# A bidirectional mLSTM layer on Trainium2: the head norm moved into the output stage, per head and 512 tokens

## The chip, the cores and the metric

The kernel runs on one core of a Trainium2 chip. The metric is the device time of one execution in microseconds (us); the median of the runs shown before the change is 2925.31 us. The engines are TensorE (PE; its weight loads are shown as PEld), VectorE (DVE), ScalarE (ACT), GpSimd (POOL) and SyncE (SP), which issues nearly all DMAs.

## The reference

One encoder layer is applied to two sequences that share all weights: a prompt of 1024 tokens and a sample of 2048 tokens, model width 1024. 16 learned meta tokens are put ahead of each. Everything is float32.

```
xn   = rmsnorm(h) ; proj = xn @ w_in + b_in          # 1024 -> 6672 columns
ya   = neighbourhood_attention(na_q, na_k, na_v) * silu(na_z) @ w_a
q, k = split(silu(conv3(ml_qk)))                     # 4 heads of 128
hm   = mlstm(q, k, v, gates) forward + the same backward
hm   = sigmoid(ml_o) * hm
hm   = (hm - mean(hm)) * rsqrt(var(hm) + eps)        # over the 128 of one head
yb   = (hm * head_g * silu(ml_z)) @ w_b
y    = (sigmoid(ga) * ya + sigmoid(gb) * yb) @ w_out
out  = h + rmsnorm(y)
```

The change concerns the three lines from `sigmoid(ml_o)` to `head_g * silu(ml_z)`: the output gate, the norm over one head, the head weights and the second gate.

## The kernel before

Two generators are woven into one program. The **dense** side does the projections and the final blocks: PLAN lists groups of columns for 1024 tokens (m: mLSTM columns, n: attention columns, g: merge gates) and, marked "f", final blocks of 512 tokens. The order is prompt m and n, sample m and n, prompt g, the prompt's final blocks f(0,0) and f(0,1), the rest of the sample, then f(1,0) to f(1,3). The **sparse** side does, in this order, the prompt's mLSTM, the prompt's neighbourhood attention (NA), the sample's mLSTM, the sample's NA. Every `yield` of the sparse side names how many us of dense PE work are to be put in before it goes on (A_D in the states stage, A_A in the output stage, A_N in the norm stage, A_NA in NA). PE executes in exactly this written order. The order of DVE, ACT and SP is chosen when the program is built; each of these engines then also runs in its order, so a waiting instruction holds back those behind it.

Every float32 product is made of three matmuls with operands split into a high and a low part (L144 to L146, L412 to L414, L1305 to L1307). The weights' parts stream from DRAM through four buffers (`whi`, `wlo`, issued at L231 when a buffer comes free). A projection unit ends in a pj bank of PSUM (three of them), which ACT or DVE evacuates; results go to DRAM (`mk`, `mq`, `nk`, ...), and the sparse side loads them again. The first group of a half of 512 tokens also stores its activation parts (`xh`, `xl`, L317).

The mLSTM of a sequence runs per head: `ml_states` (yields A_D) walks backwards over blocks of 256 tokens and leaves the chunk states, and `ml_outputs` (4 + 6 x (NB + 1) yields of A_A for NB blocks, NB being 4 or 8) walks forward. In each of its steps of six yields it makes the scores of block b (`scores`, `scores_lo`, with decay masks `um` loaded from DRAM), the products of block b - 1 with the states and with v (`back`: PE into banks tr and sm, ACT to `tt`, DVE adds into `num`), and `finish` divides by `den` into `hb`, stored to H in DRAM. The parts `vh`, `vl` of v (in `kv`) and `cch`, `ccl` of the states (in `state`) have two buffers each and are made a block ahead.

After all four heads, `ml_norm` runs as a stage of its own (1 + 5 N + 2 yields of A_N, N being 4 or 8, at 717 to 771 us for the prompt and 1930 to 2014 us for the sample): it loads H, TO (tanh of half the output gate) and SZ (the second gate) for 128 tokens and all heads, gates (L1179), takes means and variances (L1181, L1183), the inverse root (`rsqrt8`, L126 to L136), normalises (L1193), multiplies by SZ (L1194), transposes on PE (L1205), and ACT copies (L1206) to `ybo`, which is stored to YB. The head weights are in SZ already: `tm_store` multiplies each projected tile of SZ by them (L438; `hgb`, loaded in `tm_unit`).

A final block begins with `yload`, which loads YA and YB and splits them (ACT L1248, DVE L1249). It is started during the previous final block, one piece after each of its 16 output tiles, once NA and mLSTM have marked the 512 tokens done; if they never do in that time, the block loads at its own start.

```
            while acc > 0.0:
                d = next(dense, None)
...
                    elif self.ready(*nxt[1:]):
                        hook = self.yload(*nxt[1:])
```

Of the kernel before, what the change touches and what calls it, by code (L numbers as in the profile page):

```python
# [9 lines left out]
F32 = mybir.dt.float32  # L10
# [97 lines left out]
A_NA, A_D, A_A, A_N, A_G = 1.52, 1.63, 1.63, 1.85, 1.3  # L108


class K:
# [55 lines left out]
    def setup2(self):  # L167
# [10 lines left out]
        nc.vector.tensor_scalar(self.cw[:, 12:24], self.cw[:, 12:24], S_K, None, op0=ALU.mult)  # L178
        self.ones = cp.tile([P, P], F32, name="ones")
# [9 lines left out]
        self.H = [t(f"h{s}", [SEQLEN[s], 512]) for s in range(2)]  # L189
# [197 lines left out]
    def tm_unit(self, col, halves, wd):  # L387
# [4 lines left out]
        if C_MZ <= col < C_MO:  # L392
            hg = wp.tile([P, 1, 256], F32, name="hgb", bufs=1)
            nc.sync.dma_start(hg[:, 0, :], _bc(self.i["head_g"], col - C_MZ, wd))
            nc.vector.tensor_scalar(hg, hg, -0.125, None, op0=ALU.mult)
            self.hgt = hg
# [29 lines left out]
    def tm_store(self, col, wd, s, n, cnt, tok, st):  # L426
# [6 lines left out]
        if C_MZ <= col < C_MO:  # L433
# [3 lines left out]
            for a in range(2):  # L437
                nc.vector.tensor_tensor(st[:, a, :wd], st[:, a, :wd], self.hgt[:, 0, :], op=ALU.mult)  # L438
# [422 lines left out]
    def ml(self, s):  # L861
        tc, nc = self.tc, self.nc
        T = SEQLEN[s]
        NB = T // BL
        with tc.tile_pool(name=f"mg{s}", bufs=1, side="right", reuse_waits="tile") as keep:
            with tc.tile_pool(name=f"mt{s}", bufs=1, side="right", reuse_waits="tile") as mp:
                self.tri = keep.tile([P, 2, P], F32, name="tri")
                nc.sync.dma_start(self.tri, self.i["tri"])
                self.trim = keep.tile([P, 2, CB, P], F32, name="trim")
                for j in range(CB):  # L870
                    nc.sync.dma_start(self.trim[:, :, j, :], self.i["trimask"])
                g = []
                yield from self.ml_gates(s, keep, mp, g)
            with tc.tile_pool(name=f"ml{s}", bufs=1, side="right", reuse_waits="tile") as mp:
                self.vas = [mp.tile([P, CB, 130], F32, name=f"va{j}") for j in range(3)]
                for va in self.vas:
                    nc.gpsimd.memset(va[:, :, 128:129], 1.0)
                    nc.gpsimd.memset(va[:, :, 129:130], 0.0)
                for h in range(4):
                    sts = {}  # L880
                    yield from self.ml_states(mp, s, h, g, NB, sts)
                    yield from self.ml_outputs(mp, s, h, g, NB, sts)
        with tc.tile_pool(name=f"mn{s}", bufs=1, side="right", reuse_waits="tile") as mp:
            yield from self.ml_norm(mp, s)
# [103 lines left out]
    def ml_outputs(self, mp, s, h, g, NB, sts):  # L988
# [3 lines left out]
        raws, kfs, vas, ums, convs, qs, kss, vs, shs, cs, nums = ({} for _ in range(11))  # L992

        def load(b):
            if b < NB:
# [6 lines left out]
                for d in range(2):  # L1002
                    um = mp.tile([P, CB, P], F32, name="um", bufs=4)
                    ud = self.UD[s][d]
                    src = bass.AP(tensor=ud.tensor, offset=ud.offset + ((1 + b * CB) * 4 + h) * P, ap=[[0, P], [4 * P, CB], [1, P]])
                    nc.sync.dma_start(um, src)
                    ums[b].append(um)

# [19 lines left out]
        def kv(b):  # L1028
            if b < NB:
                kf, va = kfs.pop(b), vas.pop(b)  # L1030
# [4 lines left out]
                vh = mp.tile([P, CB, 130], F32R, name="vh", bufs=2)  # L1035
                vl = mp.tile([P, CB, 130], F32R, name="vl", bufs=2)
                nc.scalar.activation(f2(vh), f2(va), AF.Copy)
                nc.vector.tensor_tensor(f2(vl), f2(va), f2(vh).bitcast(F32), op=ALU.subtract)
                kss[b], vs[b] = (kh, kl), (vh, vl)
# [8 lines left out]
        def state(b):  # L1048

            if b < NB:  # L1050
                for j in range(CB):
# [5 lines left out]
                cch = mp.tile([P, CB, 260], F32R, name="cch", bufs=2)  # L1057
                ccl = mp.tile([P, CB, 260], F32R, name="ccl", bufs=2)
# [22 lines left out]
        def back(b, j):  # L1081
# [6 lines left out]
            tt = mp.tile([P, 2, 130], F32, name="tt", bufs=1)  # L1088
            for d in range(2):
                nc.scalar.activation(tt[:, d], pi[:, 130 * d:130 * d + 130], AF.Copy, scale=g[d]["e"][:, cc, h:h + 1])  # L1090
# [3 lines left out]
            if j == 0:  # L1094
                nums[b] = mp.tile([P, CB, 2, 130], F32, name="num", bufs=1)
            num = nums[b]
            nc.vector.tensor_tensor(num[:, j].rearrange("p d c -> p (d c)"), pa[:, :260], tt.rearrange("p d c -> p (d c)"), op=ALU.add)

        def finish(b):
# [27 lines left out]
        state(0)  # L1127
        yield A_A
        for b in range(NB + 1):
            p = b - 1  # L1130
            if b < NB:
                scores(b)
                conv_a(b + 1)
# [19 lines left out]
            state(b + 1)  # L1153
            yield A_A

    def ml_norm(self, mp, s):

        nc = self.nc
        N = SEQLEN[s] // (2 * P)
        ld, hs, rr = {}, {}, {}  # L1160

        def load(i):
            if i < N:
                ld[i] = []
                for e in range(2):
                    rows = slice((2 * i + e) * P, (2 * i + e + 1) * P)
                    hb = mp.tile([P, 4, P], F32, name="hn", bufs=6)
                    to = mp.tile([P, 4, P], F32, name="tog", bufs=4)
                    sz = mp.tile([P, 4, P], F32, name="szg", bufs=4)
                    for x, dr in ((hb, self.H), (to, self.TO), (sz, self.SZ)):  # L1170
                        nc.sync.dma_start(x.rearrange("p a b -> p (a b)"), dr[s][rows, :])
                    ld[i].append((hb, to, sz))

        def stats(i):
            bs = mp.tile([P, 2, 4, 6], F32, name="bs", bufs=2)
            mv = mp.tile([P, 2, 4, 2], F32, name="mv", bufs=2)
            for e in range(2):
                hb, to, _ = ld[i][e]
                nc.vector.scalar_tensor_tensor(hb, to, 1.0, hb, op0=ALU.add, op1=ALU.mult)  # L1179
                for h in range(4):  # L1180
                    nc.vector.bn_stats(bs[:, e, h], hb[:, h])  # L1181
                for h in range(4):
                    nc.vector.bn_aggr(mv[:, e, h], bs[:, e, h])  # L1183
                yield A_N
            ve = mp.tile([P, 2, 4], F32, name="ve", bufs=2)
            nc.vector.tensor_scalar(ve, mv[:, :, :, 1], 4.0 * EPS, None, op0=ALU.add)
            rr[i] = mv, self.rsqrt8(mp, ve, [P, 2, 4])

        def norm(i, e):
            mv, r = rr[i]  # L1190
            hb, _, sz = ld[i][e]
            for h in range(4):
                nc.vector.tensor_scalar(hb[:, h], hb[:, h], mv[:, e, h, 0:1], r[:, e, h:h + 1], op0=ALU.subtract, op1=ALU.mult)  # L1193
            nc.vector.tensor_tensor(hb, hb, sz, op=ALU.mult)  # L1194

        def turn(i, e):
            if i < 0:
                return
            hb = ld[i][e][0]
            if e == 0:  # L1200
                rr[i] = mp.tile([P, 4, 2, P], F32, name="ybo", bufs=2)
            yo = rr[i]
            pt = self.psum("tr", [P, 4, P])
            for h in range(4):
                nc.tensor.transpose(pt[:, h, :], hb[:, h], self.ident)  # L1205
            nc.scalar.activation(yo[:, :, e, :], pt, AF.Copy)  # L1206
            if e:
                for h in range(4):
                    nc.sync.dma_start(self.YB[s][h][:, 2 * P * i:2 * P * (i + 1)], yo[:, h].rearrange("p a b -> p (a b)"))
                ld.pop(i)  # L1210
                rr.pop(i)

        load(0)
        yield A_N
        for i in range(N + 1):
            if i < N:
                load(i + 1)
                yield from stats(i)
                yield A_N
            turn(i - 1, 0)  # L1220
            if i < N:
                norm(i, 0)
            yield A_N
            turn(i - 1, 1)
            if i < N:
                norm(i, 1)
            yield A_N
        self.done.add(("ml", s))
# [265 lines left out]
```

## Time and profile before

| what | value |
|---|---|
| median of three runs (lowest to highest) | 2925.31 us (2923.33 to 2926.53) |
| the profiled execution: its time, its span | 2927.06 us, 2925.1 us |
| PE busy, DVE busy, ACT busy (share of the span) | 97%, 60%, 44% |
| mean granted TensorE clock | 0.986 |
| DMA queue q1, share of 16 engines | 669.41 MB, 70.0% |

The span runs from the first to the last instruction of the profiled execution; the rest of its time lies around that. Busy times are unions over an engine's instructions. Matmuls are pipelined and their ends are modelled, so PE's 97% says that PE is nearly always occupied, not that it is at its peak. Where PE is not waiting, a 512-column matmul starts every 0.23 us, a 256-column one every 0.12 us.

### The profile page before, as it was taken

Reading aid. Unit: us, or ns where it says so; the run is one execution under the profiler, and the core shown is the slowest. Engines: PE = TensorE matmul, PEld = TensorE weight load, DVE = VectorE, ACT = ScalarE, POOL = GpSimd, SP = SyncE. Lnnn points to the kernel's source line nnn. Section 1 sums busy time; section 2 is a strip of 40 time slices with the busy share of each in tenths; the row PEclk is TensorE's granted clock in tenths of the full one; section 3 lists DMA queues with packets and bytes.
Section 4 is the critical chain, followed back from the end, with each engine's and each line's share of the span. In section 5 each row is a group of like instructions: output and inputs, shape, how many; then the busy total and the mean of one; then the engine's idle time right before and its main releaser. Section 6 shows DMA issues by size and latency. Waiting matters only on the chain.

```text
span 2925.1 us, 49552 instructions
## 1 busy us (share of the span) xinstructions
PE 2824.3 (97%) x17488; PEld 2514.2 (86%) x17488; DVE 1745.3 (60%) x4722; ACT 1287.4 (44%) x3114; POOL 23.0 (1%) x107
## 2 busy tenths in 40 slices
PE   6999999999799999899999999999999999999998
PEld 6998898899689988798887998888888888979877
DVE  5233566556556765466558786565555557786843
ACT  4112546443344444356566554523444445544421
POOL 1000000000000000000000000000000000000000
PEclk9999999999899999999999999999999999999999
DMA  9655566755775654469669898578569659797875
GB/s 348 222 174 184 194 224 235 251 180 195 254 248 155 200 167 142 138 219 312 212 213 356 279 346 281 154 261 273 178 190 298 192 163 289 249 303 242 274 245 194
DMA packets 438760, 675.26 MB, mean 231 GB/s; under 512 B 52240, under 2 KB 253024, under 8 KB 438512
## 3 DMA queue, kind: packets, MB, share of 16 engines
q1 hardware_dynamic: 437392, 669.41, 70.0%
q0 software_dynamic: 1120, 2.69, 0.4%
q8 instruction: 138, 2.26, 0.3%
q14 instruction: 110, 0.90, 0.1%
HBM read 455.05 MB, written 216.90 MB: 230 GB/s over the span
## 4 chain that ended last, share of the span: by engine, by line
PE 82%; DMA 9%; DVE 5%; ACT 1%; SPq 1%; issue 1%; ACTq 0%; DVEq 0%
PE pj L144 14%; PE pj L145 14%; PE pj L146 14%; PE pj L412 6%; PE pj L413 6%; PE pj L414 6%; PE pj L1305 3%; PE pj L1307 3%; PE pj L1306 3%; PE sm L702 3%; PE tr L690 3%; DMA tg<-gt 1%; PE sc L665 1%; PE sc L666 1%; PE sm L146 1%; DMA um<-ud 1%
## 5 line engine op out<-in xcount | busy, mean ns | idle before, releaser
L144 PE MATMUL pj<-xh,whi 128*128 128x512 f32 (+1 forms) x1824 | 722.3, 396 | 1.0 <-DVE xl L310 1.0
L145 PE MATMUL pj<-xl,whi 128*128 128x512 f32 (+1 forms) x1824 | 702.3, 385 | 0.1
L146 PE MATMUL pj<-xh,wlo 128*128 128x512 f32 (+1 forms) x1824 | 700.5, 384 | 0.0
L412 PE MATMUL pj<-whi,xh 128*128 128x256 f32 (+3 forms) x1576 | 451.0, 286 | 0.0
L413 PE MATMUL pj<-wlo,xh 128*128 128x256 f32 (+3 forms) x1576 | 444.6, 282 | 0.0
L414 PE MATMUL pj<-whi,xl 128*128 128x256 f32 (+3 forms) x1576 | 444.1, 282 | 0.0
L146 PEld LDWEIGHTS pj<-xh,wlo 128*128 128x128 f32 x1824 | 345.5, 189 | 72.3
L144 PEld LDWEIGHTS pj<-xh,whi 128*128 128x128 f32 x1824 | 346.0, 190 | 55.9 <-DVE xl L310 1.2
L145 PEld LDWEIGHTS pj<-xl,whi 128*128 128x128 f32 x1824 | 346.5, 190 | 53.2 <-DVE xl L310 0.4
L412 PEld LDWEIGHTS pj<-whi,xh 128*128 128x128 f32 (+1 forms) x1576 | 294.3, 187 | 1.2
L413 PEld LDWEIGHTS pj<-wlo,xh 128*128 128x128 f32 (+1 forms) x1576 | 294.0, 187 | 1.0
L414 PEld LDWEIGHTS pj<-whi,xl 128*128 128x128 f32 (+1 forms) x1576 | 293.9, 187 | 0.9
L673 ACT ACTIVATE prb<-sc,mx 128x384 f32<-128x384 f32 (+2 forms) x192 | 120.1, 625 | 237.4 <-DVE mx L669 236.3
L1305 PE MATMUL pj<-whi,mh 128*128 128x256 f32 x768 | 221.7, 289 | 2.7 <-DVE yo L1333 2.7
L1307 PE MATMUL pj<-whi,mlo 128*128 128x256 f32 x768 | 217.7, 283 | 0.0
L1306 PE MATMUL pj<-wlo,mh 128*128 128x256 f32 x768 | 217.4, 283 | 0.0
L669 DVE CUSTOM_DVE_ANT_1 sc<-sc,gt 128x384 f32<-128x384 f32 (+2 forms) x192 | 118.9, 619 | 96.3 <-PE sc L666 86.8
L708 DVE TENSOR_TENSOR yg<-sm,yg 64x128 f32<-64x128 f32 x384 | 108.4, 282 | 108.0 <-ACT yg L706 100.2
L421 DVE TENSOR_TENSOR stT<-pj,bb 128x256 f32<-128x256 f32 (+3 forms) x197 | 83.2, 422 | 143.8 <-PE pj L414 142.7
L144 PE MATMUL pj<-yh,whi 128*128 128x512 f32 x384 | 158.3, 412 | 8.5 <-ACT yh L1248 6.1
L693 DVE TENSOR_TENSOR pts<-tr,pts 96x512 fp32r<-96x512 f32 (+2 forms) x192 | 131.6, 685 | 47.8 <-ACT pts L692 46.0
L145 PE MATMUL pj<-yl,whi 128*128 128x512 f32 x384 | 153.9, 401 | 0.2 <-DVE yl L1249 0.2
(234 smaller groups left out, 5074.6 us busy)
## 6 DMA issues: line engine op xcount, KB each, us to landing
whi<-wh SPq DMA_DIRECT2D x176, 512.0 KB
wlo<-wl SPq DMA_DIRECT2D x176, 512.0 KB
wh<-whi SPq DMA_DIRECT2D x64, 512.0 KB
wl<-wlo SPq DMA_DIRECT2D x64, 512.0 KB
wraw<-w_in SPq DMA_DIRECT2D x48, 512.0 KB
gt<-st SPq DMA_DIRECT2D x96, 256.0 KB
tg<-gt SPq DMA_DIRECT2D x96, 256.0 KB
xh<-xh SPq DMA_DIRECT2D x6, 2048.0 KB
```

The lines of the kernel that those rows point to most:

```text
L144: mm(out, ah, bh, start=start, stop=False)
L145: mm(out, ah, bl, start=False, stop=False)
L146: mm(out, al, bh, start=False, stop=stop)
L412: nc.tensor.matmul(o, xh, wh, start=k == 0, stop=False)
L413: nc.tensor.matmul(o, xh, wl, start=False, stop=False)
L414: nc.tensor.matmul(o, xl, wh, start=False, stop=k == KT - 1)
L669: nc.vector.tensor_tensor_reduce(out=so, in0=so, in1=gt[:, g0:g0 + ns, c0:c0 + 32], op0=ALU.add, op1=ALU.min, scale=-1.0, scalar=3.0e38, a ...
L673: nc.scalar.activation(pr_[:, :N].rearrange("p (b a c) -> p b a c", b=4, c=8), sc[:, :N].rearrange("p (a b c) -> p b a c", b=4, c=8), AF.E ...
L693: nc.vector.tensor_tensor(pts[:ks, :, 1, :], pt[:ks], pts[:ks, :, 0, :].bitcast(F32), op=ALU.subtract)
L1305: nc.tensor.matmul(o, mh[:, k, xs], wh, start=k == 0, stop=False)
L1306: nc.tensor.matmul(o, mh[:, k, xs], wl, start=False, stop=False)
L1307: nc.tensor.matmul(o, ml[:, k, xs], wh, start=False, stop=k == KT - 1)
```

## The change

The norm stage is dissolved. `finish` now collects two blocks (512 tokens) of one head in `hb`, and every second block hands a small generator `ml_norm` to a queue. Each further yield of the output stage, or of the next head's states, runs one step of it: gate and statistics, inverse root, normalise and second gate, two empty steps, then four transposes, one ACT copy and one store to YB. TO and SZ are loaded per head and 512 tokens (`gates`), in pieces of 512 bytes a row. H is gone.

The head weights are no longer multiplied into SZ: they are a per-partition scale (`hg`, times -0.125) of the ACT copy behind the transposes, where a partition is a channel of the head.

`back` lets ACT write the state part straight into `num`, and DVE adds in place (`tt` is gone). `vh`, `vl`, `cch` and `ccl` have one buffer each and are made in the last yield of the block that they belong to, `state(b)` instead of `state(b + 1)`; the split of v moves there from `kv`. A_A is 1.9 instead of 1.63, A_N is gone. The removed lines are the old `ml_norm`, `hgb` and L438, described above.

```diff
-A_NA, A_D, A_A, A_N, A_G = 1.52, 1.63, 1.63, 1.85, 1.3
+A_NA, A_D, A_A, A_G = 1.52, 1.63, 1.9, 1.3
...
+        self.hg = cp.tile([P, 4], F32, name="hg")
+        nc.sync.dma_start(self.hg, i["head_g"].rearrange("(h p) -> p h", p=P))
+        nc.vector.tensor_scalar(self.hg, self.hg, -0.125, None, op0=ALU.mult)
...
-            for a in range(2):
-                nc.vector.tensor_tensor(st[:, a, :wd], st[:, a, :wd], self.hgt[:, 0, :], op=ALU.mult)
...
+                norm = iter(())
                 for h in range(4):
                     sts = {}
-                    yield from self.ml_states(mp, s, h, g, NB, sts)
-                    yield from self.ml_outputs(mp, s, h, g, NB, sts)
-        with tc.tile_pool(name=f"mn{s}", bufs=1, side="right", reuse_waits="tile") as mp:
-            yield from self.ml_norm(mp, s)
+                    for cost in self.ml_states(mp, s, h, g, NB, sts):
+                        next(norm, None)
+                        yield cost
+                    norms = deque()
+                    for cost in self.ml_outputs(mp, s, h, g, NB, sts, norms):
+                        if next(norm, "end") == "end" and norms:
+                            norm = norms.popleft()
+                        yield cost
+                    if norms:
+                        for _ in norm:
+                            pass
+                        norm = norms.popleft()
+                for _ in norm:
+                    yield A_A
+        self.done.add(("ml", s))
...
+        def gates(b):
+
+            if b % 2:
+                tzs[b // 2] = [mp.tile([P, 4, P], F32, name=n, tag="tz", bufs=2) for n in ("tog", "szg")]
+                for x, d in zip(tzs[b // 2], (self.TO, self.SZ)):
+                    nc.sync.dma_start(x, d[s][(b - 1) * BL:(b + 1) * BL, h * P:(h + 1) * P].rearrange("(c p) f -> p c f", p=P))
...
         def state(b):
 
             if b < NB:
+                va = vas.pop(b)
+                vh = mp.tile([P, CB, 130], F32R, name="vh", bufs=1)
+                vl = mp.tile([P, CB, 130], F32R, name="vl", bufs=1)
...
-                cch = mp.tile([P, CB, 260], F32R, name="cch", bufs=2)
-                ccl = mp.tile([P, CB, 260], F32R, name="ccl", bufs=2)
+                cch = mp.tile([P, CB, 260], F32R, name="cch", bufs=1)
+                ccl = mp.tile([P, CB, 260], F32R, name="ccl", bufs=1)
...
             for d in range(2):
-                nc.scalar.activation(tt[:, d], pi[:, 130 * d:130 * d + 130], AF.Copy, scale=g[d]["e"][:, cc, h:h + 1])
+                nc.scalar.activation(num[:, j, d], pi[:, 130 * d:130 * d + 130], AF.Copy, scale=g[d]["e"][:, cc, h:h + 1])
...
+            nj = num[:, j].rearrange("p d c -> p (d c)")
+            nc.vector.tensor_tensor(nj, pa[:, :260], nj, op=ALU.add)
...
-            hb = mp.tile([P, CB, P], F32, name="hb", bufs=2)
+            q, a = b // 2, CB * (b % 2)
+            if not a:
+                hbs[q] = mp.tile([P, 2 * CB, P], F32, name="hb", bufs=2)
+            hb = hbs[q]
             for j in range(CB):
-                nc.scalar.activation(hb[:, j], num[:, j, 0, 0:P], AF.Copy, scale=den[:, j, 0:1])
-                nc.vector.scalar_tensor_tensor(hb[:, j], num[:, j, 1, 0:P], den[:, j, 1:2], hb[:, j], op0=ALU.mult, op1=ALU.add)
-            nc.sync.dma_start(self.H[s][t0:t0 + BL, h * P:(h + 1) * P].rearrange("(c p) f -> p c f", p=P), hb)
+                o = hb[:, a + j]
+                nc.scalar.activation(o, num[:, j, 0, 0:P], AF.Copy, scale=den[:, j, 0:1])
+                nc.vector.scalar_tensor_tensor(o, num[:, j, 1, 0:P], den[:, j, 1:2], o, op0=ALU.mult, op1=ALU.add)
+            if a:
+                norms.append(self.ml_norm(mp, s, h, q, hbs.pop(q), tzs.pop(q)))
             for x in (shs, vs, qs, ums):
...
+            if p >= 0:
+                gates(p)
...
-            state(b + 1)
+            state(b)
             yield A_A
...
+    def ml_norm(self, mp, s, h, q, hb, tz):
 
         nc = self.nc
+        to, sz = tz
+        nc.vector.scalar_tensor_tensor(hb, to, 1.0, hb, op0=ALU.add, op1=ALU.mult)
+        bs = mp.tile([P, 4, 6], F32, name="bs", bufs=1)
+        mv = mp.tile([P, 4, 2], F32, name="mv", bufs=1)
+        for j in range(4):
+            nc.vector.bn_stats(bs[:, j], hb[:, j])
+        for j in range(4):
+            nc.vector.bn_aggr(mv[:, j], bs[:, j])
+        yield
+        nc.vector.tensor_scalar(mv[:, :, 1], mv[:, :, 1], 4.0 * EPS, None, op0=ALU.add)
+        rs = self.rsqrt8(mp, mv[:, :, 1], [P, 4])
+        yield
+        for j in range(4):
+            nc.vector.tensor_scalar(hb[:, j], hb[:, j], mv[:, j, 0:1], rs[:, j:j + 1], op0=ALU.subtract, op1=ALU.mult)
+        nc.vector.tensor_tensor(hb, hb, sz, op=ALU.mult)
+        yield
+        yield
+        yield
+        pt = self.psum("tr", [P, 4, P])
+        for j in range(4):
+            nc.tensor.transpose(pt[:, j, :], hb[:, j], self.ident)
+        nc.scalar.activation(hb, pt, AF.Copy, scale=self.hg[:, h:h + 1])
+        nc.sync.dma_start(self.YB[s][h][:, 512 * q:512 * q + 512], hb.rearrange("p a b -> p (a b)"))
```

More of the change, by code (lines that the diff above doesn't have):

```diff
@@ L188, in setup2 @@
         self.KF = [[t(f"kf{s}{p}", [P, SEQLEN[s]]) for p in range(4)] for s in range(2)]
-        self.H = [t(f"h{s}", [SEQLEN[s], 512]) for s in range(2)]
         self.MQ = [[t(f"mq{s}{p}", [P, NM + SEQLEN[s]]) for p in range(4)] for s in range(2)]
@@ L391, in tm_unit @@
         nc.sync.dma_start(bb[:, :wd], _bc(self.i["b_in"], col, wd))
[L392 to L396, printed above, removed]
         todo = []
@@ L986, in ml_states, with ml_outputs @@
             yield A_D
-    def ml_outputs(self, mp, s, h, g, NB, sts):
+    def ml_outputs(self, mp, s, h, g, NB, sts, norms):
         nc = self.nc
         f2 = lambda x: x.rearrange("p c t -> p (c t)")
-        raws, kfs, vas, ums, convs, qs, kss, vs, shs, cs, nums = ({} for _ in range(11))
+        raws, kfs, vas, ums, convs, qs, kss, vs, shs, cs, nums, tzs, hbs = ({} for _ in range(13))
         def load(b):
@@ L1029, in kv @@
             if b < NB:
-                kf, va = kfs.pop(b), vas.pop(b)
+                kf = kfs.pop(b)
                 kh = mp.tile([P, CB, P], F32R, name="kh", tag="kh", bufs=2)
@@ L1034, in kv @@
                 nc.vector.tensor_tensor(f2(kl), kf, f2(kh).bitcast(F32), op=ALU.subtract)
[L1035 to L1039, printed above, removed]
+                kss[b] = kh, kl
         def decay(b, d):
@@ L1050, in state @@
             if b < NB:
+                va = vas.pop(b)
+                vh = mp.tile([P, CB, 130], F32R, name="vh", bufs=1)
+                vl = mp.tile([P, CB, 130], F32R, name="vl", bufs=1)
+                nc.scalar.activation(f2(vh), f2(va), AF.Copy)
+                nc.vector.tensor_tensor(f2(vl), f2(va), f2(vh).bitcast(F32), op=ALU.subtract)
+                vs[b] = vh, vl
                 for j in range(CB):
@@ L1087, in back @@
             self.mm3(pi[:, :260], qh[:, j, :], ql[:, j, :], cch[:, j], ccl[:, j])
-            tt = mp.tile([P, 2, 130], F32, name="tt", bufs=1)
+            if j == 0:
+                nums[b] = mp.tile([P, CB, 2, 130], F32, name="num", bufs=1)
+            num = nums[b]
             for d in range(2):
-                nc.scalar.activation(tt[:, d], pi[:, 130 * d:130 * d + 130], AF.Copy, scale=g[d]["e"][:, cc, h:h + 1])
+                nc.scalar.activation(num[:, j, d], pi[:, 130 * d:130 * d + 130], AF.Copy, scale=g[d]["e"][:, cc, h:h + 1])
             pa = self.psum("sm", [P, 512])
@@ L1093, in back @@
                 self.mm3(pa[:, 130 * d:130 * d + 130], sh[:, d, j, :], sl[:, d, j, :], vh[:, j, :], vl[:, j, :])
[L1094 to L1097, printed above, removed]
+            nj = num[:, j].rearrange("p d c -> p (d c)")
+            nc.vector.tensor_tensor(nj, pa[:, :260], nj, op=ALU.add)
         def finish(b):
@@ L1126, in ml_outputs @@
         decay(0, 1)
-        state(0)
         yield A_A
@@ L1152, in ml_outputs @@
             decay(b + 1, 1)
-            state(b + 1)
+            state(b)
             yield A_A
-    def ml_norm(self, mp, s):
+    def ml_norm(self, mp, s, h, q, hb, tz):
         nc = self.nc
[L1159 to L1228, printed above, removed]
```

## The prediction

> **What bounds the kernel now.** I read the page's engine totals first, then who TensorE (PE) waited for, then busy time by stage, then the costs of single instructions.
>
> ```profile
> span 2925.1 us, 49552 instructions
> PE 2824.3 (97%) x17488; PEld 2514.2 (86%) x17488; DVE 1745.3 (60%) x4722; ACT 1287.4 (44%) x3114; POOL 23.0 (1%) x107
> ...
> PE pj L307 <- DVE xr L296: 22.6, 2, 18.3
> PE sc L665 <- ACT kd L645: 10.6, 1, 10.6
> PE tr L690 <- DVE prb L682: 9.8, 3, 6.4
> PE tr L1205 <- DVE hn L1194: 7.3, 2, 5.3
> PE pj L144 <- ACT yh L1248: 6.1, 3, 4.4
> PE sm L146 <- DVE ktl L957: 5.6, 6, 2.3
> ...
> DVE um L1044 <- DMA um<-ud: 31.0, 13, 4.2
> ```
>
> PE is busy 97% and executes in the order written; every other engine only matters where PE waits for it. The PE lines (whole run) show total wait, times, longest: the largest is the start of the program, the second the start of the first neighbourhood attention (NA), the fourth the norm stage that the change dissolves, the fifth the start of the last final block. The last line is of VectorE (DVE) between 1440 and 1810 us: it stood 31 us waiting for a load while the final blocks of the prompt ran beside the mLSTM.
>
> ```profile
> 731.00:742.00 11.00, 5.67 (x19) 4.45 (x18) 9.82 (x56) 3.24 (x6) 0.00 (x0) 0.70 0.76 275
> 742.00:772.00 30.00, 29.02 (x154) 24.05 (x154) 22.82 (x82) 11.30 (x21) 0.00 (x0) 1.00 0.56 186
> 772.00:788.00 16.00, 16.00 (x71) 12.81 (x69) 7.54 (x17) 5.65 (x10) 0.00 (x0) 1.00 1.05 371
> 788.00:806.00 18.00, 7.09 (x22) 5.11 (x20) 2.93 (x4) 3.94 (x6) 0.00 (x0) 0.72 0.82 267
> 1552.00:1642.00 90.00, 84.19 (x508) 74.26 (x508) 78.59 (x184) 57.79 (x153) 0.12 (x2) 0.98 0.99 346
> 2806.00:2830.00 24.00, 17.63 (x76) 13.16 (x76) 11.52 (x29) 4.10 (x9) 0.00 (x0) 0.79 0.73 241
> ```
>
> Columns: stretch, length, busy us of PE, weight loads, DVE, ACT, POOL, granted clock, DMA share, GB/s. Each long wait of PE (731, 788, 2812) goes with a lower clock; the tightest stretch for DVE is 1552 to 1642, 87% busy with the DMA engines at 0.99.
>
> **What stays the same.** The built programs have the same multiset of PE instructions: 24 groups of four norm transposes before and after. So PE's own work is worth zero, and the whole question is where PE waits.
>
> **Pace of the schedule.** A yield hands the dense side so many us of PE work. The old norm stage had 23 and 43 yields of 1.85: 122.1 us of budget, gone. The output stage has 4 heads x (34 + 58) = 368 yields, each 0.27 dearer: +99.4. Four yields of 1.90 drain the last norm of each sequence: +15.2. Sum -7.5: the prompt's mLSTM ends 1.7 us later against the dense work, the whole sparse side 7.5 us earlier.
>
> **The norm stage's waits go: -10.** Its two waits at L1205 are 7.3 us of idle PE. The matmuls after the first are slower too: from start to start, intervals exceed the medians of their forms by 7.9 us in sum between 731 and 742, and by 2.2 around the second wait at 1943. Taken: -10; with idle time alone, -7. Inside the output stage a norm's transposes come three steps (some 6 us of PE) after its multiply, so I expect no new wait there where DVE has room.
> By the Trainium skill ("TensorE: Matmul & The Clock Gate", Part 1) an idle window of about 3.4 us halves the clock for at least another: the 5.3 us wait would cost some 1.7 us more, the 2.0 us wait nothing, and this term would be -9.0; the trace's 0.70 clock at 731 to 742 and 2.2 us agree roughly.
>
> **The last final block: -8.** Its inputs are fetched once the last NA tile is done. Following the loops with the new costs, this happens three tile steps earlier (24 matmuls of 0.12 us, 2.9 us each): five steps before the block instead of two, so the 6.1 us at L1248 are covered by 8.6 us more lead. With its slow clock the place costs more: intervals exceed their medians by 9.9 us up to 2825. Bounds: -3, if the loads then queue behind the block's weights; -12, if the later wait for tg (2.1) goes as well. Taken -8.
>
> **Start of the first NA: +5.5.** This is the step that speaks against the change. SP issues DMAs in one order. Before, the q and k loads stood behind the saved activations (xh, xl: 4.2 MB), one weight pair (1.05 MB) and a store; from the issue of xh (773.8) to the landing of kr (some 797.5) 6.1 MB took 23.8 us. In the changed program's SP order two more weight pairs, two more stores, the output gain and a yb store stand ahead: 9.5 MB to the same point. With 1.3 MB in flight, at 312 GB/s (772 to 797) that is 34.7 us; xh is issued some 16 us ahead of the first score (before: 14), which gives a wait of 18 us against 10.6. At the best rate seen, 371, it is 13; if the extra loads were issued early enough to be gone, the last store that gates SP, 3 to 4 us ahead of the score, still leaves about 4.5. So -6 to +10; nearest to the row is the loaded queue: +5.5.
>
> **DVE in the output stage: 0, from -8 to +18.** One step block (256 tokens, a head) by the group means: two conv steps 0.96, q's gate and the low parts of q, k and v 4 x 0.42, the decay masks 0.85, states 0.70, ccl 0.69, scores 1.67, num 0.85, den 0.64, hb 0.70: 8.7 us.
>
> ```profile
> L1179 DVE SCALAR_TENSOR_TENSOR hn<-tog,hn 128x512 f32<-128x512 f32 x24 | 16.5, 687 | 9.3 <-DMA tog<-to 4.6 <-DMA hn<-h 2.9 <-issue 1.3
> L1181 DVE BATCH_NORM_STATS2 bs<-hn 128x6 f32<-128x128 f32 x96 | 21.2, 278 | 0.1
> L1183 DVE BATCH_NORM_AGGREGATE mv<-bs 128x2 f32<-128x6 f32 x96 | 10.2, 157 | 0.0
> L1193 DVE TENSOR_SCALAR hn<-hn,mv,nwy 128x128 f32<-128x128 f32 x96 | 25.6, 340 | 0.1
> L1194 DVE TENSOR_TENSOR hn<-hn,szg 128x512 f32<-128x512 f32 x24 | 15.7, 682 | 0.0
> ```
>
> Busy us, then mean ns, then idle before. A norm is 0.69 + 4 x 0.28 + 4 x 0.16 + 12 small ones of 0.16 + 4 x 0.34 + 0.68 = 6.4 us per two blocks, 3.2 each. A block lasts 6 x 1.63 + 2.7 us of its own matmuls = 12.5 us, afterwards 6 x 1.90 + 2.9 = 14.3. DVE: 70% before, (8.7 + 3.2) / 14.3 = 83% after. Alone that fits. Beside the first half of a final block, whose DVE work (L1284 twice, L1286, L1288: 2.74 us per 24 matmuls of 0.235) adds 49% of the dense share, it is 122%; as a 685 ns instruction is followed by the next after 603, some 108%. Before it was about 95% beside outputs and more beside the states, where L957 cost PE 5.6 us. That overlap is some 56 us for each of the prompt's two final blocks: 4 to 5 us of overload each, about what the two free pj banks (2.8 us each) hold. On the other side the um loads move ahead of the stores that held them back (31 us of DVE waits), the states no longer meet the tightest part, and 48 multiplications at L438 (18 us, all beside dense work that waits for nothing) are gone; I set these against each other.
>
> **The rest: +1.** The 24 products of head weights are free in the scale of an ACT copy (L1206, 598 ns, same count). H's stores and loads (12.6 MB) go, against gate rows read in pieces of 512 bytes instead of 2 KB: 30 ns a packet against 93 for four times the bytes, which 16 engines feel as 10 us over the whole run, less than H's own 41; ACT writing straight into num removes a buffer, not an instruction. The single vh, vl, cch, ccl buffers make the splits wait for the previous block's last matmul; from there to their first use lie four steps, 8.3 us of PE, against 0.42 + 0.42 + 0.64 + 0.69 of splitting, which the built DVE order puts right behind that matmul's addition. If DVE is late there, up to 2 us per block would show. Bounds 0 to +6 (three late blocks); taken +1, as PE waits nowhere for DVE between 1290 and 1375, where DVE is 66% busy.
>
> **Sum.** -10 - 8 + 5.5 + 0 + 1 = -11.5. The profiled run took 2927.06 around its span of 2925.1; that is 1.75 above the median of the three, 2925.31. Against the median: 2914 us. A difference of 0.2%, 5.9 us, is about what a measurement here can tell from none.
>
> **Rivals.** (a) As above: 2914, own range 2904 to 2919; 55%. (b) DVE becomes the bound beside the prompt's two final blocks: if the um waits stay, 31 us in 370, 8% are added to the 108%, PE stretches by 16% of 112 us = 18 us, and the sum is +6.5: 2932, more if the first NA takes its upper value. It decides as soon as demand and waits together pass what the two banks hold. For it: 87% busy at 1552 to 1642 with PE waiting; against: DVE idles for DMA there, not from work. 25%. (c) The start of the first NA eats the gain: at the 258 GB/s of its own row, 9.5 MB take 37 us, the wait is 21, +10 instead of 5.5, and with the tail at its small end, -3, the sum is -2: 2923. 13%. (d) The change does not do what it says, it hides nothing: the norm's waits come back at its 24 transposes, 0.4 us each (the six waits of L957 have a mean of 0.9), which gives 2923. 7%.
>
> **Numbers.** Faster is (a), 55%; same is (c) and (d), 20%; slower is (b), 25%. The range 2902 to 2937 takes in (a) with the low ends of NA and tail, and most of (b).
>
> **What would show it.** Right: no wait at the norm's transposes, the wait for yh (L1248 before) under 2 us, the clock at full speed near 2820, the first NA score waiting 13 to 20 us, and PE waits between 1440 and 1810 no more than today's 7 us. Wrong: waits of PE for ccl, sl, tg or hb in that stretch summing to over 15 us, or DVE over 92% busy there.

## The result, and the profile after

The changed kernel takes 3001.85 us (median of 4 runs, 2997.44 to 3007.64) against 2924.32 for the kernel before: ratio 1.0268, 95% interval 1.0252 to 1.0284. It is 78 us slower, where I had forecast 11 us faster and a range that ended at 2937. Line numbers below are the changed kernel's where nothing else is said.

The page of the changed kernel, first lines and engine totals (busy us, share, instructions):

```profile
span 2995.7 us, 49364 instructions
PE 2831.6 (95%) x17488; PEld 2519.5 (84%) x17488; DVE 1759.0 (59%) x4813; ACT 1293.0 (43%) x3114; POOL 23.2 (1%) x107
```

PE executes the same number of matmuls and is busy 7 us more, DVE 14 us more; the span grew by 70.6 us. So nearly all of the loss is time in which PE stands. Who it waited for in the changed kernel (total, times, longest), whole run:

```profile
PE tr L1201 <- DVE hb L1195: 67.0, 12, 10.9
PE pj L309 <- DVE xr L298: 22.9, 2, 18.6
PE sc L660 <- ACT kd L640: 13.9, 1, 13.9
PE tr L685 <- DVE prb L677: 11.3, 6, 4.1
PE tr L1201 <- ACT hb L1130: 6.6, 1, 6.6
PE sm L749 <- DVE g_lf L743: 6.5, 1, 6.5
PE sc L660 <- ACT prb L668: 3.8, 3, 1.7
PE tr L1201 <- DVE den L1122: 3.7, 1, 3.7
```

L1201 is the norm's four transposes, L1195 its last DVE instruction, the product with szg. With one more wait of 1.2 us the four rows of L1201 hold 78.5 us in 15 waits, against 7.3 in the kernel before (its L1205). Three of these rows name another instruction, but in all 15 waits the transposes start 0.15 us after the product's end, so all are waits for it. The longest ones change the clock as well. The same columns as before: stretch, length, busy us of PE, weight loads, DVE, ACT, POOL, granted clock, DMA share, GB/s:

```profile
384.00:402.00 18.00, 10.53 (x91) 10.32 (x89) 15.35 (x61) 8.68 (x25) 0.10 (x1) 0.89 0.67 207
402.00:406.00 4.00, 3.90 (x23) 3.77 (x24) 0.43 (x1) 0.69 (x1) 0.00 (x0) 0.63 0.51 164
430.00:434.00 4.00, 3.75 (x32) 3.78 (x33) 1.09 (x5) 1.63 (x5) 0.00 (x0) 1.00 0.98 326
1560.00:1690.00 130.00, 91.20 (x490) 78.96 (x489) 96.35 (x276) 61.98 (x147) 0.10 (x1) 0.84 0.81 272
1634.00:1654.00 20.00, 9.10 (x49) 7.76 (x48) 18.50 (x63) 9.91 (x28) 0.00 (x0) 0.75 0.81 275
```

Behind a wait of 7.6 us, which ended at 402, PE runs at 0.63 of its clock for 4 us; behind one of 2.8 us, which ended at 430, it runs at full clock. All nine waits at the transposes of 3.7 us and more carry a stretch of half clock, none of the six shorter ones does; the clock records of the whole run sum to 139 us at half clock against 83 before. The rule of the Trainium skill that the prediction weighed ("TensorE: Matmul & The Clock Gate", Part 1: an idle window of about 3.4 us lowers the clock) agrees with these fifteen waits. Shorter waits are not safe, though: in the kernel before, waits of 1.8, 2.0, 2.7 and 2.1 us, which end at 819, 1230, 2643 and 2854, are each followed by 3.4 us at half clock.

Between 1560 and 1690 PE loses 39 of 130 us, while DVE is busy 74%. So DVE is not the bound on average; it is late at one place, and while PE stands there DVE works off its queue (92% busy from 1634 to 1654, around the longest wait). What DVE did for the first norm, in order (start, duration, idle time before in brackets):

```profile
384.33 0.61 DVE L1131 SCALAR_TENSOR_TENSOR hb<-num,den,hb 128x128 f32<-128x128 f32 x2
...
385.52 0.68 DVE L1182 SCALAR_TENSOR_TENSOR hb<-tog,hb 128x512 f32<-128x512 f32 x1
386.12 0.75 DVE L1088 TENSOR_TENSOR um<-um,sc 128x256 f32<-128x256 f32 x2
386.79 0.48 DVE L851 SCALAR_TENSOR_TENSOR cv<-raw,cw,cv 128x256 f32<-128x256 f32 x1
387.18 0.87 DVE L1186 BATCH_NORM_STATS2 bs<-hb 128x6 f32<-128x128 f32 x4
...
390.28 0.17 DVE L1190 TENSOR_SCALAR mv<-mv 128x4 f32<-128x4 f32 x1
...
394.05 0.42 DVE L1054 TENSOR_TENSOR um<-um,trim 128x256 f32<-128x256 f32 x1 [2.51 <-DMA um<-ud]
394.39 0.48 DVE L851 SCALAR_TENSOR_TENSOR cv<-raw,cw,cv 128x256 f32<-128x256 f32 x1
394.79 0.16 DVE L135 SCALAR_TENSOR_TENSOR nwy<-nwt,nwy 128x4 f32<-128x4 f32 x1
...
399.31 1.12 DVE L1194 TENSOR_SCALAR hb<-hb,mv,nwy 128x128 f32<-128x128 f32 x4
400.34 0.35 DVE L1131 SCALAR_TENSOR_TENSOR hb<-num,den,hb 128x128 f32<-128x128 f32 x1
...
401.26 0.69 DVE L1195 TENSOR_TENSOR hb<-hb,szg 128x512 f32<-128x512 f32 x1
```

And PE in the same time:

```profile
394.25 0.28 PE L411 MATMUL pj<-whi,xl 128*128 128x256 f32 x1
402.10 1.09 PE L1201 MATMUL tr<-ident,hb 128*128 128x128 f32 x4 [7.57 <-DVE hb L1195]
```

The norm's 26 DVE instructions are some 6 us of work, as the prediction had it. They take 16.4 us, from 385.52 to 401.95, because each needs the one before, and DVE runs its queue in order: between them stand the next block's convolution, scores, state splits and one wait of 2.5 us for a um load. That queue does not follow the source: the next block's L1131, at 400.34, stands three steps behind the product with szg (L1195) in the code and runs ahead of it. PE is at the transposes at 394.5, 9.0 us after the norm's first DVE instruction, and stands there with dense matmuls behind it. Over the 24 norms the chain takes 6.1 to 18.0 us, PE comes 3.4 to 13.5 us after its start, and in 15 of them PE is there first.

The other marks: the first NA score waits 13.9 us (before 10.6; forecast 13 to 20); the waits for yh of the last final block are 2.8 us (before 6.1; forecast under 2), and the clock there is 0.83 (2890 to 2900), not full; DVE's waits for um between 1440 and 1810 are 13.4 us (before 31.0). The sign of being wrong that the prediction named did show: PE's waits for hb between 1440 and 1810 sum to 41.8 us, where 15 was the mark.

### The profile page after: what moved, and what is told of

It reads as the page before. It is cut to its first block, busy times and chain, and to the rows that moved or that the text cites. A ratio compares the mean times of both kernels' runs of the same rounds, so it can differ in the third digit from the quotient of the medians.

```text
span 2995.7 us, 49364 instructions
## 1 busy us (share of the span) xinstructions
PE 2831.6 (95%) x17488; PEld 2519.5 (84%) x17488; DVE 1759.0 (59%) x4813; ACT 1293.0 (43%) x3114; POOL 23.2 (1%) x107
## 4 chain that ended last, share of the span: by engine, by line
PE 43%; DVE 6%; DMA 6%; ACT 1%; issue 1%; SPq 0%; DVEq 0%; ACTq 0%
PE pj L144 9%; PE pj L145 9%; PE pj L146 9%; PE pj L1280 2%; PE pj L1282 2%; PE pj L1281 2%; PE sm L697 2%; PE tr L685 2%; DMA tg<-gt 1%; DMA um<-ud 1%; DMA yr<-yb 1%; PE sc L660 1%; PE sc L661 1%; PE sm L146 1%; PE pj L409 1%
```

## The experiments

Two theories to begin with. **Late chain:** the loss is latency, the norm's chain ends after PE gets to its transposes. **Overload:** DVE has too much to do in the output stage, and the transposes are only where it shows. **Single buffers** and **pace** stood beside them. Later the question was what is left once the chain has time. Each ratio below is to the kernel before, run in the same round; its median lies between 2918.5 and 2924.3 us in the different rounds, so experiments of different rounds are compared by their ratios. Each trace is one execution.

**1. Transposes five steps later (e1_lag5).**

```diff
         nc.vector.tensor_tensor(hb, hb, sz, op=ALU.mult)
         yield
-        yield
-        yield
+        for _ in range(7):
+            yield
         pt = self.psum("tr", [P, 4, P])
```

> Each norm's transposes come five more steps after its multiply (11 steps after the norm is handed over instead of 6); the instructions are the same. Theory 1, late chain: the loss is latency; in the changed kernel's trace the norm's serial chain on DVE (gate product, statistics, inverse root, normalise, multiply) ends 1 to 11 us after PE, which runs in order, has reached the transposes, in 12 of 24 norms, while DVE is only 74% busy between 1560 and 1690 us. Five steps are some 12 us, more than the longest wait of 10.9: PE's 78.5 us of waits at the transposes go to under 5, and the time falls from 3001 to 2917 to 2930. Theory 2, overload: DVE has too much to do in the output stage, and the transposes are only where it shows; then waits of the same sum come back at the products of scores, states and numerators, and the time stays above 2970. Theory 3, single buffers: the splits of v and of the states start a block late and the norm queues behind them; the transposes' waits go, waits at the state and score products come (20 us or more), 2940 to 2960.

Measured: 2925.95 us, 1.0012 of the kernel before (1.0002 to 1.0023). Who PE waited for, rows of the norm's transposes in the whole run; then the one stretch in which it still did:

```profile
PE tr L1201 <- DVE hb L1195: 12.7, 2, 11.3
```

```profile
1549.00:1577.00 28.00, 16.73 (x91) 14.33 (x90) 28.00 (x85) 16.04 (x39) 0.00 (x0) 0.88 0.95 343
```

By the ratios some 75 of the 78 us are back, and in the source only the place of 96 transposes has changed. The chains last as long as before (11.5 us in the mean of 24, in both kernels), but PE now comes 21.5 us after their start in the mean instead of 9.2. 22 of 24 norms no longer wait. The waits left are 12.7 us where under 5 were expected: one norm waits 11.3 us, and there the reading is another. DVE is busy for 28 us without a gap, and that norm's chain takes 26 us.

**2. Two steps later (e2_lag2).** The same edit with `range(4)`.

> Two more steps (some 4.8 us of PE) between multiply and transposes instead of five. Late chain: taking 4.8 us from each of the twelve long waits (7.6, 2.8, 8.7, 6.6, 10.5, 9.1, 10.9, 8.3, 3.7, 5.0, 1.8, 1.3 us) leaves some 28 us, so the time falls by about 48, to 2950 to 2960, between the changed kernel and the one with five steps. Overload: what is taken from the transposes comes back elsewhere; above 2980. Single buffers: 2960 to 2980.

Measured: 2964.91 us, 1.0157 (1.0133 to 1.0180). Waits of the transposes:

```profile
PE tr L1201 <- DVE hb L1195: 53.2, 7, 17.6
```

In between, as the late chain has it, but 5 us above the expected 2950 to 2960, and 53 us of waits are left where taking 4.8 us from each left 28. The chain gives some of the time back: the fifteenth norm waits 17.6 us here and 10.9 in the changed kernel. A likely reason is that a standing PE hands DVE no new work either, so that where PE stands less, the queue is longer; no run isolates that.

**3. The wait cut (e3_uncouple).**

```diff
-            nc.tensor.transpose(pt[:, j, :], hb[:, j], self.ident)
-        nc.scalar.activation(hb, pt, AF.Copy, scale=self.hg[:, h:h + 1])
-        nc.sync.dma_start(self.YB[s][h][:, 512 * q:512 * q + 512], hb.rearrange("p a b -> p (a b)"))
+            nc.tensor.transpose(pt[:, j, :], self.ident, self.ident)
+        nc.scalar.activation(to, pt, AF.Copy, scale=self.hg[:, h:h + 1])
+        nc.sync.dma_start(self.YB[s][h][:, 512 * q:512 * q + 512], to.rearrange("p a b -> p (a b)"))
```

> The norm's work on DVE stays as it is and PE's transposes stand where they were, but they turn the identity tile instead of the norm's result, and ACT writes them into the gate's tile; the norm's result is left out of the output. Late chain: nothing waits for the chain's end, PE's waits at the transposes vanish, 2917 to 2930. Overload: DVE's work is the same, so its backlog stops PE elsewhere; above 2970. If it comes out well above the five-step kernel, the norm's multiply also holds up the loads of its next gates.

Measured: 2912.43 us, 0.9969 (0.9958 to 0.9980), below the expected 2917 to 2930. PE's largest waits in it, the program's start left out (tg is the merge gate of a final block):

```profile
PE sc L660 <- ACT kd L640: 14.7, 1, 14.7
PE tr L685 <- DVE prb L677: 10.9, 5, 2.6
PE pj L144 <- DVE tg L1259: 7.4, 5, 2.9
```

PE's order is that of the changed kernel and DVE has the same instructions (in another order at 425 of 4813 places); the dependence of PE on the chain is gone, and by the ratios some 87 us with it. This settles that the loss is that wait. A full DVE alone does not stop PE: between 1549 and 1577 DVE has no gap here either (28.00 of 28.00 us), and PE has none (28.00). It is also the kernel that the prediction described, one whose norms make nobody wait: its forecast of 2914 against 2925.31 is a ratio of 0.9961.

**4. The old pace (e4_pace163).**

```diff
-A_NA, A_D, A_A, A_G = 1.52, 1.63, 1.9, 1.3
+A_NA, A_D, A_A, A_G = 1.52, 1.63, 1.63, 1.3
```

> The output stage's yields hand the dense side 1.63 us as in the kernel before, instead of 1.90; all else as in the changed kernel. Late chain: the five steps before the transposes hold 5 x 0.27 = 1.4 us less of PE's work, so each of some 15 late norms waits 1 to 1.5 us more: slower than the changed kernel, 3010 to 3030. Theory 4, pace: the dearer steps push the sparse side to meet dense work that it does not fit beside, and the norms only show it; then the time falls back to within 20 us of the kernel before, under 2945.

Measured: 3021.55 us, 1.0348 (1.0333 to 1.0364). Two of the transposes' rows:

```profile
PE tr L1201 <- DVE hb L1195: 82.8, 14, 12.1
PE tr L1201 <- DVE den L1123: 14.7, 3, 6.0
```

With shorter steps PE comes earlier; 20 norms wait instead of 15, 108 us in sum instead of 78.5, and the time is in the range expected of the late chain. The dearer steps were a help, not the harm.

**5. and 6. Fourteen steps, and DVE relieved (e5_lag14, e6_lag14_relief).** The transposes go to a list of their own, so that the next norm starts on time. In the second kernel the inverse root also takes two steps of three (with the constant in `hg` changed to fit; not shown), and the normalisation goes to ACT:

```diff
-        for j in range(4):
-            nc.vector.tensor_scalar(hb[:, j], hb[:, j], mv[:, j, 0:1], rs[:, j:j + 1], op0=ALU.subtract, op1=ALU.mult)
+        nb = mp.tile([P, 4], F32, name="nb", bufs=1)
+        nc.vector.scalar_tensor_tensor(nb, mv[:, :, 0], -1.0, rs, op0=ALU.mult, op1=ALU.mult)
+        for j in range(4):
+            nc.scalar.activation(hb[:, j], hb[:, j], AF.Identity, scale=rs[:, j:j + 1], bias=nb[:, j:j + 1])
```

> Transposes 14 steps after the hand-over of the norm (changed kernel 6, five-step kernel 11), through a list of its own so that the next norm starts on time. In the five-step kernel one norm still waits 11.3 us at 1576 us, in a stretch (1549 to 1577) where DVE is busy without a gap: its chain takes 26 us there. Late chain alone: 14 steps are some 33 us, all waits at the transposes go, and the time comes to that of the kernel whose transposes read the identity, 2912 (2908 to 2918). Local overload (rival b of the prediction): the backlog of the stretch is work that DVE has to do before PE can go on; PE waits there elsewhere, at tg, mlo or ktl, by 8 to 12 us more, and the time stays at 2920 to 2927.

> As the 14-step kernel, with DVE relieved: the four normalisations (4 x 0.34 us) go to ACT (4 x 0.39, bias from one small DVE product) and the inverse root takes two steps of three, some 1.7 us less DVE work per norm, 7% of what DVE does per two blocks. Late chain alone: nothing waits for the norm any more, so relief changes nothing: within 3 us of the 14-step kernel. Local overload: 5 to 6 us of DVE work leave the stretch from 1516 to 1600, and PE's waits there shrink by 3 to 6 us.

Measured: 2925.88 us, 1.0006 (0.9996 to 1.0017), and 2920.23 us, 0.9988 (0.9977 to 1.0000). The one wait of the transposes that is left, in the first (each with the line numbers of its own kernel):

```profile
PE tr L1207 <- DVE hb L1202: 16.3, 1, 16.3
```

and in the second:

```profile
PE tr L1209 <- DVE mv L1195: 10.5, 1, 10.5
```

More distance alone brings nothing beyond five steps: the same norm is now 35 us under way (1558.6 to 1594.0), DVE is busy 34.4 of them, and PE, at the transposes at 1577.8, still arrives first. Less DVE work takes 5.8 us from the wait and 5.7 us (0.18%) from the time, which is near the bound of what can be told from nothing. So in this one stretch, where the first final block meets the output stage, DVE holds the norm up by its load; no other norm waits. The expectation had the wait move to other places; it stayed at the transposes. The relief also makes the chain itself shorter, so the cause is not shown by this run alone; the last run leaves the chain as it is.

**7. and 8. Two parts of the change alone, in the kernel before (e7_before_single, e8_before_headw).** In the first, vh, vl, cch and ccl with `bufs=1`, split in `state(b)`, which follows one block later. In the second, hgb and its 48 products go, and the copy out of the transposes carries the weights:

```diff
-            nc.scalar.activation(yo[:, :, e, :], pt, AF.Copy)
+            for h in range(4):
+                nc.scalar.activation(yo[:, h, e, :], pt[:, h, :], AF.Copy, scale=self.hg[:, h:h + 1])
```

> The kernel before, with one part of the change alone: single vh, vl, cch and ccl buffers, split one block later (norm stage and head weights as before). The prediction put this at +1 us, 0 to +6. If single buffers were part of the loss (theory 3): PE waits for ccl, cch, vl or vh, 10 us or more. Late chain: 2921 to 2928, no such waits over 2 us in sum.

> The kernel before, with one part of the change alone: head weights applied as the scale of ACT's copy out of the norm's transposes (four copies of 128x128 here, since the four heads stand in one tile), and 48 products of 128x256 less on DVE beside the gate projections. The prediction put it at nothing: 2919 to 2928. If DVE's work beside the projections did hold PE up, it is 5 to 15 us faster.

Measured: 2921.69 us, 0.9993 (0.9982 to 1.0004), and 2918.86 us, 0.9982 (0.9972 to 0.9993). The single buffers cost nothing: PE waits 0.6 us in sum for vh and vl, and not at all for cch and ccl. The head weights in ACT's copy are worth 0.18%, some 5 us: little, but the interval leaves out 1, and the prediction had put it at nothing.

**9. to 11. The weight splits on POOL (e9_lag5_pool, e10_before_pool, e11_lag14_relief_pool).** The prediction's DVE sum for 1500 to 1600 had left out that the first final block is the first to use its weights, so DVE splits them (L238, 1.22 us per 24 matmuls). POOL is idle:

```diff
-                eng = nc.vector if self.nu > 4 else nc.gpsimd
+                eng = nc.vector if self.nu > 4 and key[0] == "i" else nc.gpsimd
```

> The five-step kernel with the low parts of the 16 weight tiles of the final blocks (first used by the prompt's first final block) split on POOL, which is idle, instead of DVE: 1.2 us each on DVE, 2.4 us on POOL by the rows of the program's start. The prediction's DVE sum for the stretch from 1500 to 1600 left these splits out: one per 24 matmuls (5.6 us) beside the 2.74 us it counted. Local overload: the backlog that holds one norm up by 11.3 us at 1576 melts by 8 to 12 us of DVE work; the wait goes under 3 us and the time falls by 7 to 12, to 2914 to 2919. Late chain without overload: the DVE queue is not full because of these splits; the wait stays at 8 us or more and the time within 3 us of the five-step kernel, 2923 to 2929. If POOL's accesses slow DVE (a 128x512 product over 0.75 us instead of 0.68), it is slower than that.

> The same 16 splits moved to POOL in the kernel before. PE waits some 5 us more than its medians there between 1500 and 1600 and 6 between 1600 and 1700. Local overload is a matter of the norms added to that stretch: here DVE has room, and the time falls by 0 to 4 us (2919 to 2923). If the splits cost PE in any schedule: 6 us or more.

> The 14-step kernel with the relief (normalise on ACT, two root steps) and the 16 splits on POOL. Local overload: the last long wait (10.5 us) goes and with it 8 to 12 us: 2908 to 2914, faster than the kernel before by 0.3% or more. Late chain without overload: 2917 to 2922.

Measured: 2928.76 us, 1.0033 (1.0020 to 1.0046); 2924.29 us, 1.0014 (1.0001 to 1.0026); 2925.12 us, 1.0033 (1.0020 to 1.0047). All three times missed. The waits did shrink, from 11.3 to 6.6 us at that norm in the first, and no norm waits for its chain in the third; the kernels were no faster for it. The profiled execution of the first took 2921.59 us, the fastest of its five. Three groups of it (duration ns min/median/max):

```profile
L238 POOL TENSOR_TENSOR wlo<-wraw,whi x19: 2338/2405/3227, 11.1 to 1628.2; 128x1024 fp32r<-128x1024 f32 x19
L1195 DVE TENSOR_TENSOR hb<-hb,szg x24: 670/684/2872, 402.2 to 2001.9; 128x512 f32<-128x512 f32 x24
L1261 DVE TENSOR_TENSOR tg<-tg x48: 665/684/2875, 1534.2 to 2865.7; 128x512 f32<-128x512 f32 x48
```

The medians of the two DVE lines are what they were; some single instructions last up to 2.9 us (in the five-step kernel at most 0.693). One of them, in order of time, DVE and then POOL:

```profile
1570.15 0.67 DVE L1259 SCALAR_TENSOR_TENSOR tg<-tg,pj 128x512 f32<-128x512 f32 x1
1570.75 2.23 DVE L1195 TENSOR_TENSOR hb<-hb,szg 128x512 f32<-128x512 f32 x1
```

```profile
1569.21 3.23 POOL L238 TENSOR_TENSOR wlo<-wraw,whi 128x1024 fp32r<-128x1024 f32 x1 [3.31 <-ACT whi L235]
```

The product ends 0.54 us after POOL's split, as if it had begun only then. L1259, which takes one operand from PSUM, ran meanwhile at its usual 0.67. The Trainium skill ("SBUF — State Buffer", SBUF: two separate sides) says that a DVE operation with two SBUF inputs and a POOL operation that reads SBUF hold their shared ports exclusively, the second one waiting for the end of the first. This trace agrees, with 2.23 us for 0.68. In the whole trace the 15 DVE instructions that overlap a moved split and last over 0.1 us longer than their medians are 23.6 us longer in sum, against 19.5 us of splits taken off DVE (16 x 1.22). The work had not left DVE's time, it blocked it; the overload could not be measured in this way.

**12. The splits left out (e12_lag5_nosplit).**

```diff
-                eng.tensor_tensor(lo[:, :n], raw[:, :n], hi[:, :n].bitcast(F32), op=ALU.subtract)
+                if key[0] == "i":
+                    eng.tensor_tensor(lo[:, :n], raw[:, :n], hi[:, :n].bitcast(F32), op=ALU.subtract)
+                else:
+                    lo = hi
```

> The five-step kernel without the 16 subtractions that split the final blocks' weight tiles (16 x 1.22 = 19.5 us of DVE work, half of it between 1500 and 1600); nothing is moved to another engine, the high part is used in place of the low part, so the output leaves the low parts of these weights out. The run with the splits on POOL could not measure the overload: there DVE products with two operands in SBUF lasted up to 2.9 us instead of 0.68, until POOL's 2.4 us splits ended. Local overload: the wait of 11.3 us at the norm's transposes at 1576 goes to under 3, and the time falls by 7 to 13 us against the five-step kernel (2926, 1.0012 of the kernel before), to about 0.997 to 0.999 of the kernel before. Late chain without overload: the wait stays at 8 us or more, 1.000 to 1.002.

Measured: 2920.22 us, 0.9993 (0.9983 to 1.0004). The stretch that had 16.73 us of PE and 28.00 of DVE in the five-step kernel:

```profile
1549.00:1577.00 28.00, 26.20 (x133) 21.31 (x133) 25.03 (x73) 17.25 (x42) 0.00 (x0) 1.00 1.05 368
```

No norm waits any more; the chain of the one that did takes 15.8 us instead of 26.2, with the same instructions in it. By the ratios (1.0012 to 0.9993) the time falls by some 5.6 us, less than the 7 to 13 expected: part of the wait comes back where the final block waits for tg (5.5 us between 1440 and 1810, 2.0 in the five-step kernel). So the last wait comes from DVE's load and not from the distance. It is worth some 6 us, the size that the relief found; the two intervals just overlap, so the wait that went is the firmer evidence. Lateness is worth the 75 of the first run.

## Why the prediction was wrong

- **PE's own work, zero:** right, 17488 matmuls in both.
- **"The norm stage's waits go: -10 ... a norm's transposes come three steps (some 6 us of PE) after its multiply, so I expect no new wait there where DVE has room":** this is the step that failed. The old waits did go, but 78.5 us of new ones came. I took the line at which the multiply is written for the time at which it runs. PE's order follows the code; DVE's does not, and its queue puts most of a block's other work between the links of a chain of 26. The comparison to make was of two arrivals. PE came to the transposes 9.0 us after the norm's first DVE instruction in the timeline above, 9.2 in the mean of the 24 norms. The chain is 6 us of its own work plus what DVE does beside it: with 8.7 of 14.3 us of the queue taken by other work, an estimate from the prediction's numbers is 6 / (1 - 0.61) = 15 us; the first norm took 16.4, the mean of all is 11.5. The prediction held the numbers of this estimate and compared sums of work, not the two arrival times.
- **Rival (d), the waits come back at the transposes:** the mechanism that happened, with 7% and priced at 0.4 us each from the mean of L957's waits. It was 3.3 us for each of the 24 norms (78.5 / 24). The row it was priced from is a single DVE instruction behind a matmul; this is a chain.
- **Rival (b), DVE the bound beside the prompt's final blocks:** true of one norm, at 1576 us. Its demand was understated, since the splits of L238 were left out of the 2.74 us per 24 matmuls; they make it 3.96. In the kernel without the norm's wait, matmul intervals between 1500 and 1700 exceed their medians by 17.2 us against 11.4 before: the term that I took at 0 was some +6 (one execution of each).
- **Start of the first NA, +5.5:** +3.3 in the changed kernel, +4.1 without the norm's waits; right, near the low end. The size is partly luck: it hangs on the schedule, for in the five-step kernel that wait is 3.1 us, 7.5 less than before, and in the 14-step kernel it is absent.
- **The last final block, -8:** the place is right, the size about 5: the same measure after 2800 us gives 9.5 against 14.7 before, without the norm's waits. This too hangs on the schedule: the five-step kernel waits 6.3 us for yh again.
- **The rest, +1:** single buffers 0.9993, right within what can be told; head weights 0.9982, some 5 us that the prediction put at nothing.
- **The sum:** without the norm's waits the ratio is 0.9969 (0.9958 to 0.9980), against a forecast of 0.9961. That the terms agree so well in sum is partly luck: DVE's +6 and the smaller tail are made up by time elsewhere that I had not listed, such as 6 us of the stretch from 700 to 900 us (the same measure gives 29.0 before and 19.3 there; the norm stage and the NA term explain some 4 of these 10 us).

What stays open: why the one norm's chain grew from 26 to 35 us when its transposes moved three steps further. The order in which DVE's queue was built differs between the two kernels in many places, and no run holds it fixed.

## What to carry to other kernels

When a serial chain is moved from a stage of its own into a busy stage, compare two arrival times: when the in-order consumer gets there, and when the last link ends in a queue that also serves others; the chain's own work can be a third of that. Give the consumer its distance in steps of the stage and test it by one run whose consumer reads something that is ready. Distance cures lateness but not a full queue, and the share of an engine over a stage tells neither.

## What the runs showed of the hardware

- A DVE product of two SBUF operands that meets a POOL subtraction over SBUF waits for its end: up to 2.87 us instead of 0.68, with the median unchanged. With 16 subtractions moved to an idle POOL three kernels were 0.1 to 0.5% slower than their counterparts by the ratios, the smallest at the edge of what can be told.
- At the transposes of the changed kernel each of nine waits of PE of 3.7 us or more carried a stretch of half clock, none of six of 2.8 us or less did; elsewhere shorter ones did too (four of 1.8 to 2.7 us in the kernel before). The changed kernel spent 56 us more at half clock than the one before, part of it idle anyway.
